# A hybrid encoder layer on one core: the last product of the MLP adds onto accumulator rows placed in PSUM, and the closing norm is reordered

## The chip, the core and the metric

The kernel runs on one core of a Trainium2 chip. The core has five engines that run side by side, each with an instruction queue of its own: TensorE (PE) for matrix products, VectorE (DVE), ScalarE (ACT), GpSimd (POOL) and SyncE (SP), which here only starts transfers. Matrix products write to PSUM, which has eight banks of 128 partitions by 512 fp32; everything else lives in SBUF, and a store to DRAM starts from SBUF. The metric is the device time of one execution in microseconds (us). Before the change it is 755.47 us, the median of three runs (755.42 to 755.72).

## What is computed

One layer over 512 frames of width 1024, in fp32: a gated input projection, forgetting attention and a gated recurrence, an output projection, cross attention to 256 memory tokens, a squared-ReLU MLP with hidden width 4096, and a final RMS norm. Only the end matters here:

```python
u = rmsnorm(h, norm_ff_g[l]) @ w1[l]
h = h + jnp.square(jax.nn.relu(u)) @ w2[l]
return rmsnorm(h, final_norm_g)      # h * rsqrt(mean(h*h) + eps) * g, row by row
```

The output is 512 rows of 1024 numbers, 2 MB.

## The kernel before

Each fp32 operand of a product is split in a high and a low part, and a product is three matmuls (high by high, high by low, low by high). The hidden width is cut into eight groups of 512, numbered g. The MLP's products of group 1 and later use seven products of half-size blocks in place of eight, named "1" to "7" and done in the order 1, 5, 6, 2, 7, 3, 4 (`PRODUCTS`). The weights of each product come as a unit that ACT copies to its high part (line 181, tile `whd`) and DVE subtracts to its low part (line 185, tile `wld`).

The second MLP product is `mlp_down` (line 1528). The last call takes groups 6 and 7 together. A product adds into a pair of PSUM banks, one for each half `t` of 128 rows: `U` for products 1, 6, 7 and 4, `Y` for 5 and 3, `V` for 2. `PLAN` (line 1518) names, for each product, the bank and the quarters of the result that it is added to when it is done. The result is in four tiles `acc[0]` to `acc[3]` of 128 rows by 1024 columns in SBUF; `rows` 0 means tiles 0 and 1, `rows` 1 means tiles 2 and 3, and `half` is the left or right 512 columns. `add_to` (line 1511) is DVE's addition of a bank onto such a quarter. After product 7 the left halves of tiles 2 and 3 lack only what bank `U` holds plus product 4. After product 3 tiles 0 and 1 are complete.

`finish` (line 1635) runs for the products that complete a half of a tile in the last call. The first time for a tile it takes the sum of squares of that half on ACT (line 1641), adds a term for eps on POOL (line 1642) and multiplies the half by the norm's gain `gfin` on POOL (line 1644, tile `fa`). The second time, after product 3, for tiles 0 and 1, it adds the squares of the other half on DVE (`squares`, line 1605) and takes the power -1/2 on POOL (`row_scale`, line 1610, tile `fr`). Tile 0 is scaled and stored at once: `scale_a` on ACT scales the half that was multiplied by the gain already, `dma_a` stores it from ACT's queue, `scale_b` on DVE multiplies the other half by the row factor and the gain and stores it from SP's queue. Tile 1 is put into `deferred`.

`last_product` (line 1566) is product 4. Inside it the order of ACT's and DVE's instructions is the order of the program text; PE's is so everywhere. Elsewhere a scheduler orders ACT, DVE, POOL and the transfers by when it reckons that they can start and by their place in the text. The block does:

- `add_to` of bank `U` for tile 3, then twelve matmuls of 512 columns for tile 2 onto bank `U` (`product`), and `add_to` of that bank onto tile 2;
- scaling and stores of tile 1, and ACT's squares of tile 2 (line 1589);
- for each 256 columns of tile 3: twelve matmuls into a fresh bank `Z`, DVE's addition onto tile 3 (line 1598) and DVE's squares (line 1599);
- `scale_a`, `dma_a`, `scale_b` for tile 2 and then tile 3, with the gain read from a copy in PSUM (`gfin_ps`, lines 1717 and 1718).

The outputs leave in eight transfers of 256 KB, two for each tile, four from ACT's queue and four from SP's. The program's end (line 1744) waits on SP for every transfer and then joins the engines.

Of the kernel before, what the change touches and what calls it, by code (L numbers as in the profile page):

```python
# [46 lines left out]
def emit(  # L47
# [21 lines left out]
    nc = tc.nc  # L69
    te, ve, ac, gp = nc.tensor, nc.vector, nc.scalar, nc.gpsimd  # L70
# [3 lines left out]
    out = out[0]  # L74
# [22 lines left out]
    def s4(shape, name, dt=F32):  # L97
        return s4p.tile([P] + shape, dt, tag="s4", name=name)
# [556 lines left out]
    for hp in range(2):  # L655
        wt = next_panel()
        for j in range(2):
            h = 2 * hp + j
            ps = mm(f"gq{h}")
# [63 lines left out]
    for hp in range(2):  # L723
        Ac.append(t2(f"Ac{hp}", F32, (8, 64)))
        dgs = []
        for h in (2 * hp, 2 * hp + 1):
            dgs.append(sc(f"dg{h}", (4, 64)))
            for c in range(NT):
                for o in (0, 64):
                    cs = slice(c * P + o, c * P + o + 64)  # L730
# [53 lines left out]
    for li, m in enumerate(mlev):  # L784
# [8 lines left out]
        for hp in range(2):  # L793
# [3 lines left out]
            ps = sc(f"lv{hp}{m}", (NT, 2, w))  # L797
# [5 lines left out]
        for hp, ps in enumerate(lvs):  # L803
# [18 lines left out]
            for j in range(2):  # L822
                h = 2 * hp + j
                qv, kv, fv = halves(qt_(h), m), halves(kt_(h), m), halves(F_[:, j, :], m)
# [3 lines left out]
            fv = halves(F_.rearrange("p h t -> p (h t)"), m)  # L828
# [93 lines left out]
    for c in range(NT):  # L922
        cs = slice(c * P, (c + 1) * P)
# [23 lines left out]
        with ahead(P1):  # L947
            hs = sm(4, f"hs{c}")
# [136 lines left out]
    for n in range(len(pairs) + 2):  # L1085
        if n < len(pairs):
            p, tb = pairs[n]
# [165 lines left out]
    acc = []  # L1253
# [53 lines left out]
    HS = S // 2  # L1307
# [196 lines left out]
    def hidden_ahead(key, n, within=None):  # L1504

        used = hb_order.index(key)
        for k in hb_order[used : used + n]:
            if k not in hbs and k[0] in comb and (within is None or k[0] in within):
                hidden_part(*k)

    def add_to(ps, rows, half, t, sign):
        a = acc[2 * rows + t][:, half * S : (half + 1) * S]
        if sign > 0:
            ve.tensor_tensor(a, ps, a, ALU.add)
        else:
            ve.scalar_tensor_tensor(a, ps, -1.0, a, op0=ALU.mult, op1=ALU.add)
# [11 lines left out]
    def mlp_down(gs):  # L1528

        end = gs[-1] == NG - 1  # L1530
        banks = {}
        for n, name in enumerate(PRODUCTS):
            bank, first_, goes = PLAN[name]
            if end and name == PRODUCTS[-1]:
                last_product(gs, banks)
                return
            for g, t in [(g, t) for g in gs for t in range(2)]:
                whi, wlo = unit("d", g, name)
                hidden_ahead((g, name), 1)
                hb = hbs[g, name]  # L1540
                if first_ and g == gs[0]:
                    banks[bank, t] = {"U": sc, "Y": tr}[bank](f"{bank}{g}{t}")
                ps = banks[bank, t]
                ts_ = slice(t * P, (t + 1) * P)
                for k in range(2):
                    hi, lo = hb[:, 0, k, ts_], hb[:, 1, k, ts_]
                    begin = first_ and g == gs[0] and k == 0
                    te.matmul(ps, hi, whi[:, k, :], start=begin, stop=False, skip_group_check=True)  # L1548
                    te.matmul(ps, hi, wlo[:, k, :], start=False, stop=False, skip_group_check=True)  # L1549
                    at = te.matmul(ps, lo, whi[:, k, :], start=False, stop=k == 1, skip_group_check=True)  # L1550
                presum.tick(6 * S / 2400, at)
                if end and (g, t) == (gs[0], 1):
                    hidden_ahead((g, name), HB + 1)
                if g != gs[-1]:
                    continue
                if name == "1":
                    banks["V", t] = mm(f"V{g}{t}")
                    ac.activation(banks["V", t], ps, AF.Copy)
                for rows, half, sign in goes:
                    add_to(ps, rows, half, t, sign)  # L1560
                    if end and (name, rows) in FINAL:
                        finish(2 * rows + t, half)
            hidden_ahead((gs[-1], name), HB, gs)
            yield

    def last_product(gs, banks):

        name = PRODUCTS[-1]

        def steps(g, t, cols):  # L1570
            (whi, wlo), hb = unit("d", g, name), hbs[g, name]
            for k in range(2):
                hi, lo = (hb[:, x, k, t * P : (t + 1) * P] for x in range(2))
                yield from ((hi, whi[:, k, cols]), (hi, wlo[:, k, cols]), (lo, whi[:, k, cols]))

        def product(ps, t, cols, start):
            ops = [op for g in gs for op in steps(g, t, cols)]
            for i, (a, b) in enumerate(ops):
                te.matmul(ps, a, b, start=start and i == 0, stop=i == len(ops) - 1, skip_group_check=True)

        with tc.manual_schedule(engines={mybir.EngineType.Activation, mybir.EngineType.DVE}):
            add_to(banks["U", 1], 1, 0, 1, 1)
            product(banks["U", 0], 0, slice(0, S), False)
            add_to(banks["U", 0], 1, 0, 0, 1)
            o2, o3, v = s4([D], "fo2"), s4([D], "fo3"), fin[3][0]
            _, half1, o1, r1_ = deferred
            scale_a(1, o1, r1_)
            e2 = sm(1, "fv2")
            ac.activation(o2[:, 0:S], acc[2][:, 0:S], AF.Square, scale=1.0 / 32.0, accum_out=e2)
            gp.tensor_tensor(e2, e2, fin[2][0], op=ALU.add)  # L1590
            r2_ = row_scale(e2, "fr2")
            dma_a(1, o1)
            scale_b(1, half1, o1, r1_, gfin[half1])
            for q in range(2):
                qs = slice(q * HS, (q + 1) * HS)
                ps = mm(f"Z{q}")[:, 0:HS]
                product(ps, 1, qs, True)
                ve.tensor_tensor(acc[3][:, qs], ps, acc[3][:, qs], ALU.add)
                v = squares(3, o3, qs, v, f"fv3{q}")
            for tb, o, r in ((2, o2, r2_), (3, o3, row_scale(v, "fr3"))):  # L1600
                scale_a(tb, o, r)
                dma_a(tb, o)
                scale_b(tb, 0, o, r, gfin_ps)

    def squares(tb, o, cs, v0, name):
        a, v = acc[tb][:, cs], sm(1, name)
        ve.tensor_tensor_reduce(out=o[:, cs], in0=a, in1=a, scale=1.0 / D, scalar=v0, op0=ALU.mult, op1=ALU.add, accum_out=v)
        return v

    def row_scale(v, name):  # L1610
        r = sm(1, name)
        gp.tensor_tensor(r, v, mhalf[:, 0:1], op=ALU.pow)
        return r

    def rows_(tb):
        return slice(tb * P, (tb + 1) * P)

    def scale_a(tb, o, r):
        _, cs, ag = fin[tb]
        ac.activation(o[:, cs], ag, AF.Identity, scale=r)  # L1620

    def dma_a(tb, o):
        cs = fin[tb][1]
        ac.dma_start(out[rows_(tb), cs], o[:, cs])

    def scale_b(tb, half, o, r, g):
        cs = slice(half * S, (half + 1) * S)
        ve.scalar_tensor_tensor(o[:, cs], acc[tb][:, cs], r, g, op0=ALU.mult, op1=ALU.mult)
        nc.sync.dma_start(out[rows_(tb), cs], o[:, cs])


    FINAL = (("2", 0), ("7", 1), ("3", 0))
    fin, deferred = {}, []

    def finish(tb, half):

        a = acc[tb]
        cs = slice(half * S, (half + 1) * S)
        if tb not in fin:
            e = sm(1, f"fe{tb}")  # L1640
            ac.activation(t2(f"fj{tb}"), a[:, cs], AF.Square, scale=1.0 / 32.0, accum_out=e)
            gp.tensor_tensor(e, e, eps3[:, tb : tb + 1], op=ALU.add)
            ag = t2(f"fa{tb}")
            gp.tensor_tensor(ag, a[:, cs], gfin[half], op=ALU.mult)
            fin[tb] = (e, cs, ag)
            return
        o = s4([D], f"fo{tb}")
        r = row_scale(squares(tb, o, cs, fin[tb][0], f"fv{tb}"), f"fr{tb}")
        if tb == 1:

            deferred.extend((tb, half, o, r))
            return
        scale_a(tb, o, r)
        dma_a(tb, o)
        scale_b(tb, half, o, r, gfin[half])

    for g in range(1, NG):
        up_units(g)
# [55 lines left out]
                pass  # L1714

    hidden_ahead((NG - 2, PRODUCTS[0]), HB)
    gfin_ps = pvt("gfin_ps")
    ac.activation(gfin_ps, gfin[0], AF.Copy)
    for _ in mlp_down((NG - 2, NG - 1)):
        pass  # L1720

# [27 lines left out]
```

## Time and profile before

| what | value |
|---|---|
| median of three runs | 755.47 us (755.42 to 755.72) |
| the profiled execution's own time | 755.52 us |
| its span, first to last instruction | 753.8 us |
| granted TensorE clock, mean | 0.998 |
| share of PE in the chain that ended last | 95% |

The span is what the profile shows; 1.7 us of the profiled execution's time lie around it. The page of the profile gives busy times of the engines, a picture of the span in 40 slices, and the chain of work that ended last. The trace behind it can be asked for the instructions in order of time (start, duration, engine, line, operation, destination and sources), for the waits, and for each engine's busy time and the transfers' rate in any stretch. An issue is the instruction on an engine's queue that starts a transfer. Times within the span are counted from its start.

### The profile page before, as it was taken

How to read it: one execution, taken by the hardware profiler on the slowest of the kernel's cores; microseconds unless marked ns; L12 is line 12 of the kernel's file. 1: busy time of each engine (PE TensorE's matmuls, PEld its weight loads, DVE VectorE, ACT ScalarE, POOL GpSimd, SP SyncE). 2: the span in 40 equal slices, each digit the busy share in tenths (PEclk: the TensorE clock that was granted, in tenths of full speed). 3: DMA queues.
4: the chain of work that ended last, by engine and by line, in shares of the span. 5: the costliest groups of instructions: out<-in, count | busy, mean ns of one | idle time of the engine just before them, and what ended most of it. 6: DMA issues, size and time to landing. Idle time of an engine off the chain costs nothing.

```text
span 753.8 us, 12203 instructions
## 1 busy us (share of the span) xinstructions
PE 744.8 (99%) x4573; PEld 651.3 (86%) x4573; DVE 539.0 (72%) x849; ACT 434.1 (58%) x721; POOL 202.5 (27%) x278
## 2 busy tenths in 40 slices
PE   9999999999999999999999999999999999999996
PEld 6889788888888988888888889898989899999985
DVE  5647873677878756645546589978788778878797
ACT  5655555655766532334434369757666757574863
POOL 7207531233433237621011211111111111100033
PEclk9999999999999999999999999999999999999999
DMA  8641987567947889985678997998989898968352
GB/s 250 197 117 56 307 264 222 179 227 254 300 175 224 269 219 210 196 164 117 128 174 156 220 209 204 224 230 240 229 205 248 221 241 210 245 194 238 125 113 111
DMA packets 109964, 152.91 MB, mean 203 GB/s; under 512 B 6177, under 2 KB 75850, under 8 KB 109906
## 3 DMA queue, kind: packets, MB, share of 16 engines
q1 hardware_dynamic: 85314, 111.74, 45.9%
q0 software_dynamic: 24000, 39.35, 30.0%
q10 hardware_dynamic: 592, 1.05, 0.4%
q8 instruction: 36, 0.59, 0.3%
q14 instruction: 22, 0.18, 0.1%
HBM read 147.91 MB, written 51.40 MB: 264 GB/s over the span
## 4 chain that ended last, share of the span: by engine, by line
PE 95%; DVE 1%; ACT 1%; POOL 1%; issue 1%; ACTq 0%; POOLq 0%
PE U L1548 4%; PE U L1549 4%; PE U L1550 4%; PE uU L1423 4%; PE uU L1422 4%; PE uU L1421 4%; PE xq L254 2%; PE wo L254 2%; PE xq L255 2%; PE xq L256 2%; PE xw L256 2%; PE xw L255 2%; PE xw L254 2%; PE wo L256 2%; PE wo L255 2%; PE Y L1548 2%
## 5 line engine op out<-in xcount | busy, mean ns | idle before, releaser
L185 DVE TENSOR_TENSOR wld<-wrd,whd 128x1024 fp32r<-128x1024 f32 x56 | 68.3, 1222 | 15.2 <-ACT whd L181 15.1
L185 DVE TENSOR_TENSOR wlu<-wru,whu 128x1024 fp32r<-128x1024 f32 x49 | 59.0, 1218 | 26.6 <-ACT whu L181 26.6
L181 ACT ACTIVATE whu<-wru 128x1024 fp32r<-128x1024 f32 x49 | 51.7, 1060 | 44.6 <-PE U L1550 16.8
L181 ACT ACTIVATE whd<-wrd 128x1024 fp32r<-128x1024 f32 x56 | 58.9, 1052 | 10.9 <-PE uU L1422 4.8
L1548 PE MATMUL U<-whd,hb 128*128 128x512 f32 x120 | 46.8, 390 | 0.0
L1549 PE MATMUL U<-wld,hb 128*128 128x512 f32 x120 | 46.8, 390 | 0.0
L1550 PE MATMUL U<-whd,hb 128*128 128x512 f32 x120 | 46.7, 389 | 0.0
L445 POOL DMA_DIRECT2D wsd<-in_w_dram x16 | 17.4, 1085 | 79.4 <-PE U L1550 15.3
L1015 POOL TENSOR_SCALAR bi<-nF,Ft 128x128 f32<-128x128 f32 (+3 forms) x32 | 21.2, 670 | 59.8 <-PE pt L1047 33.8
L445 POOL DMA_DIRECT2D wsu<-in_w_dram x14 | 17.1, 1218 | 54.6 <-PE xw L256 15.5
L1423 PE MATMUL uU<-x_hi,wlu 128*128 128x256 f32 x112 | 31.7, 283 | 0.0
L1421 PE MATMUL uY<-xs_hi,whu 128*128 128x256 f32 x112 | 31.7, 283 | 0.0
L1422 PE MATMUL uY<-xs_lo,whu 128*128 128x256 f32 x112 | 31.7, 283 | 0.0
L1423 PE MATMUL uY<-xs_hi,wlu 128*128 128x256 f32 x112 | 31.7, 283 | 0.0
L1421 PE MATMUL uU<-xs_hi,whu 128*128 128x256 f32 x112 | 31.7, 283 | 0.0
L1422 PE MATMUL uU<-xs_lo,whu 128*128 128x256 f32 x112 | 31.7, 283 | 0.0
L1423 PE MATMUL uU<-xs_hi,wlu 128*128 128x256 f32 x112 | 31.7, 283 | 0.0
L1422 PE MATMUL uU<-x_lo,whu 128*128 128x256 f32 x112 | 31.7, 283 | 0.0
L1421 PE MATMUL uU<-x_hi,whu 128*128 128x256 f32 x112 | 31.7, 283 | 0.0
L1360 POOL DMA_DIRECT2D wrd<-in_w_dram x8 | 9.7, 1218 | 78.2 <-DVE wld L185 51.1
L1360 POOL DMA_DIRECT2D wru<-in_w_dram x7 | 9.3, 1329 | 68.2 <-DVE wlu L185 68.2
L1158 ACT ACTIVATE x_hi<-hT,gv 128x512 fp32r<-128x512 f32 x16 | 11.4, 715 | 27.5 <-DVE hT L1157 27.5
(965 smaller groups left out, 2659.8 us busy)
## 6 DMA issues: line engine op xcount, KB each, us to landing
wsd<-in_w_dram SPq DMA_DIRECT2D x24, 512.0 KB, 7.5
wrd<-in_w_dram SPq DMA_DIRECT2D x24, 512.0 KB, 5.5
wrd<-wsd SPq DMA_DIRECT2D x24, 512.0 KB, 4.3
wsu<-in_w_dram SPq DMA_DIRECT2D x21, 512.0 KB, 6.1
wru<-in_w_dram SPq DMA_DIRECT2D x21, 512.0 KB, 6.2
wru<-wsu SPq DMA_DIRECT2D x21, 512.0 KB, 5.2
wsd<-in_w_dram POOLq DMA_DIRECT2D x16, 512.0 KB, 7.7
wsu<-in_w_dram POOLq DMA_DIRECT2D x14, 512.0 KB, 7.4
```

What stands on the lines that cost most here:

```text
L181: at = ac.activation(hi, raw, AF.Copy)
L185: ve.tensor_tensor(lo, raw, f(hi), ALU.subtract)
L254: te.matmul(ps, wh, hi, start=n_ == 0 and not begun, stop=False)
L255: te.matmul(ps, wh, lo, start=False, stop=False)
L256: at = te.matmul(ps, wl, hi, start=False, stop=k == order[-1])
L445: yield gp.dma_start(wsum[kind, g, name], src, accum_op=ALU.add, **more)
L1421: te.matmul(ps[:, i, :], whi[:, k, ws], xh[:, k, :], start=begin, stop=False, skip_group_check=True)
L1422: te.matmul(ps[:, i, :], whi[:, k, ws], xl[:, k, :], start=False, stop=False, skip_group_check=True)
L1423: at = te.matmul(ps[:, i, :], wlo[:, k, ws], xh[:, k, :], start=False, stop=k == UK - 1, skip_group_check=True)
L1548: te.matmul(ps, hi, whi[:, k, :], start=begin, stop=False, skip_group_check=True)
L1549: te.matmul(ps, hi, wlo[:, k, :], start=False, stop=False, skip_group_check=True)
L1550: at = te.matmul(ps, lo, whi[:, k, :], start=False, stop=k == 1, skip_group_check=True)
```

## The change

After product 7 of the last call a new function `onto_rows` runs on DVE. It adds the left half of tile 2 onto its bank `U`, in place. It writes the sum of tile 3's bank and the right 256 columns of tile 3's left half to a PSUM bank of its own, and adds the left 256 columns of tile 3's bank onto tile 3 in SBUF. So product 4 of tile 2 ends with the finished rows in its bank, and so does product 4 of the last 256 columns of tile 3; only the first 256 columns of tile 3 are still added by DVE. Squares and scaling read these banks directly.

For tile 0 the squares go from DVE to ACT, and its `scale_b` goes into the block of `last_product`, as all of tile 1's closing does. In the block the order is by hand: product 4 of tile 2; DVE's squares of tile 1; `scale_b` of tile 0; ACT's squares of tile 2's bank; `scale_a`, store and `scale_b` of tile 1; `scale_a` of tile 2, stored from SP's queue; the first 256 columns of tile 3; `scale_b` of tile 2; the last 256 columns with ACT's squares, one DVE addition of the two sums of squares, the power, and the scaling of tile 3. The gain's copy in PSUM is gone.

The stores: `scale_b` of tiles 0 and 1 leaves in three transfers (32, 32 and 64 rows), of tile 2 in two (64 rows each), and of tile 3 in two of 256 columns each. With the four of `scale_a` there are 14 in place of 8; 11 are issued from SP's queue and 3 from ACT's.

```diff
             if end and name == "7":
+                onto_rows(banks)
...
+    def onto_rows(banks):
+        u0, u1, a = banks["U", 0], banks["U", 1], acc[3]
+        ve.tensor_tensor(u0, u0, acc[2][:, 0:S], ALU.add)
+        onto.append(mm("Z1")[:, 0:HS])
+        ve.tensor_tensor(onto[0], u1[:, HS:S], a[:, HS:S], ALU.add)
+        ve.tensor_tensor(a[:, 0:HS], u1[:, 0:HS], a[:, 0:HS], ALU.add)
...
-            add_to(banks["U", 1], 1, 0, 1, 1)
-            product(banks["U", 0], 0, slice(0, S), False)
-            add_to(banks["U", 0], 1, 0, 0, 1)
...
+            u0 = banks["U", 0]
+            product(u0, 0, slice(0, S), False)
+            o2, o3 = s4([D], "fo2"), s4([D], "fo3")
+            (half, o0, r0_), (_, o1, r1_) = deferred
+            hs = slice(half * S, (half + 1) * S)
+            row_scale(r1_, squares(acc[1][:, hs], o1[:, hs], fin[1][0], "fv1"))
+            e2, e3, r2_, r3_ = sm(1, "fv2"), sm(1, "fv3"), sm(1, "fr2"), sm(1, "fr3")
+            scale_b(0, half, o0, r0_)
+            ac.activation(o2[:, 0:S], u0, AF.Square, scale=1.0 / 32.0, accum_out=e2)
+            gp.tensor_tensor(e2, e2, fin[2][0], op=ALU.add)
+            row_scale(r2_, e2)
             scale_a(1, o1, r1_)
...
+            dma_a(ac, 1, o1)
+            scale_b(1, half, o1, r1_)
+            scale_a(2, o2, r2_)
+            dma_a(nc.sync, 2, o2)
+            h0, h1 = slice(0, HS), slice(HS, S)
+            z0, z1 = mm("Z0")[:, 0:HS], onto[0]
+            product(z0, 1, h0, True)
+            ve.tensor_tensor(acc[3][:, h0], z0, acc[3][:, h0], ALU.add)
+            v3 = squares(acc[3][:, h0], o3[:, h0], fin[3][0], "fv30")
+            scale_b(2, 0, o2, r2_, u0)
+            product(z1, 1, h1, False)
+            ac.activation(o3[:, h1], z1, AF.Square, scale=1.0 / 32.0, accum_out=e3)
+            ve.tensor_tensor(e3, e3, v3, ALU.add)
+            row_scale(r3_, e3)
+            scale_a(3, o3, r3_)
+            dma_a(ac, 3, o3)
+            for cs, src in ((h0, acc[3][:, h0]), (h1, z1)):
+                ve.scalar_tensor_tensor(o3[:, cs], src, r3_, gfin[0][:, cs], op0=ALU.mult, op1=ALU.mult)
+                nc.sync.dma_start(out[rows_(3), cs], o3[:, cs])
...
+    def scale_b(tb, half, o, r, src=None):
+        cs = slice(half * S, (half + 1) * S)
+        src = acc[tb][:, cs] if src is None else src
+        ve.scalar_tensor_tensor(o[:, cs], src, r, gfin[half], op0=ALU.mult, op1=ALU.mult)
+        n = P // 4
+        for lo, hi in ((0, n), (n, 2 * n), (2 * n, P)) if tb < 2 else ((0, 2 * n), (2 * n, P)):
+            nc.sync.dma_start(out[tb * P + lo : tb * P + hi, cs], o[lo:hi, cs])
...
+        o, r = s4([D], f"fo{tb}"), sm(1, f"fr{tb}")
+        if tb == 0:
+            v = sm(1, "fv0")
+            ac.activation(o[:, cs], a[:, cs], AF.Square, scale=1.0 / 32.0, accum_out=v)
+            gp.tensor_tensor(v, v, fin[0][0], op=ALU.add)
+            row_scale(r, v)
+            scale_a(0, o, r)
+            dma_a(ac, 0, o)
+        deferred.append((half, o, r))
...
-    gfin_ps = pvt("gfin_ps")
-    ac.activation(gfin_ps, gfin[0], AF.Copy)
```

More of the change, by code (lines that the diff above doesn't have):

```diff
@@ L1562, in mlp_down @@
                         finish(2 * rows + t, half)
+            if end and name == "7":
+                onto_rows(banks)
             hidden_ahead((gs[-1], name), HB, gs)
             yield
+    onto = []
+    def onto_rows(banks):
[4 more added lines that the diff above has]
+        ve.tensor_tensor(a[:, 0:HS], u1[:, 0:HS], a[:, 0:HS], ALU.add)
     def last_product(gs, banks):
@@ L1581, in last_product @@
         with tc.manual_schedule(engines={mybir.EngineType.Activation, mybir.EngineType.DVE}):
-            add_to(banks["U", 1], 1, 0, 1, 1)
-            product(banks["U", 0], 0, slice(0, S), False)
-            add_to(banks["U", 0], 1, 0, 0, 1)
-            o2, o3, v = s4([D], "fo2"), s4([D], "fo3"), fin[3][0]
-            _, half1, o1, r1_ = deferred
-            scale_a(1, o1, r1_)
-            e2 = sm(1, "fv2")
-            ac.activation(o2[:, 0:S], acc[2][:, 0:S], AF.Square, scale=1.0 / 32.0, accum_out=e2)
@@ L1590, in last_product @@
[L1590 to L1603, printed above, removed]
@@ L1605, in squares @@
-    def squares(tb, o, cs, v0, name):
-        a, v = acc[tb][:, cs], sm(1, name)
-        ve.tensor_tensor_reduce(out=o[:, cs], in0=a, in1=a, scale=1.0 / D, scalar=v0, op0=ALU.mult, op1=ALU.add, accum_out=v)
-        return v
-    def row_scale(v, name):
-        r = sm(1, name)
+            u0 = banks["U", 0]
[3 more added lines that the diff above has]
+            hs = slice(half * S, (half + 1) * S)
@@ new lines, in last_product, with squares @@
+            row_scale(r3_, e3)
[4 more added lines that the diff above has]
+                nc.sync.dma_start(out[rows_(3), cs], o3[:, cs])
+    def squares(a, o, v0, name):
+        v = sm(1, name)
+        ve.tensor_tensor_reduce(out=o, in0=a, in1=a, scale=1.0 / D, scalar=v0, op0=ALU.mult, op1=ALU.add, accum_out=v)
+        return v
@@ L1612, in row_scale @@
+    def row_scale(r, v):
         gp.tensor_tensor(r, v, mhalf[:, 0:1], op=ALU.pow)
@@ L1620, in scale_a, with dma_a @@
         ac.activation(o[:, cs], ag, AF.Identity, scale=r)
-    def dma_a(tb, o):
+    def dma_a(queue, tb, o):
         cs = fin[tb][1]
-        ac.dma_start(out[rows_(tb), cs], o[:, cs])
-    def scale_b(tb, half, o, r, g):
+        queue.dma_start(out[rows_(tb), cs], o[:, cs])
+    def scale_b(tb, half, o, r, src=None):
         cs = slice(half * S, (half + 1) * S)
-        ve.scalar_tensor_tensor(o[:, cs], acc[tb][:, cs], r, g, op0=ALU.mult, op1=ALU.mult)
-        nc.sync.dma_start(out[rows_(tb), cs], o[:, cs])
+        src = acc[tb][:, cs] if src is None else src
[3 more added lines that the diff above has]
+            nc.sync.dma_start(out[tb * P + lo : tb * P + hi, cs], o[lo:hi, cs])
     FINAL = (("2", 0), ("7", 1), ("3", 0))
@@ L1646, in finish @@
             return
[L1647 to L1655, printed above, removed]
+        o, r = s4([D], f"fo{tb}"), sm(1, f"fr{tb}")
[7 more added lines that the diff above has]
+        deferred.append((half, o, r))
     for g in range(1, NG):
```

## The prediction

> **What bounds the kernel now.** I read the page first (span, engines, chain), then the chain and the timeline of the last 18 us, then the waits of SP and the rate of the transfers in the tail.
>
> ```profile
> span 753.8 us, 12203 instructions
> PE 744.8 (99%) x4573; PEld 651.3 (86%) x4573; DVE 539.0 (72%) x849; ACT 434.1 (58%) x721; POOL 202.5 (27%) x278
> PE 95%; DVE 1%; ACT 1%; POOL 1%; issue 1%; ACTq 0%; POOLq 0%
> ```
>
> PE is busy for 99% of the span and makes 95% of the chain. The change keeps all its matmuls, so only two things can move: whether PE stays without a gap, and what comes after its last matmul. The chain and the timeline show that end:
>
> ```profile
> 741.32 2.72 PE U L1579 x12
> 744.04 2.88 PE Z L1579 x24
> ...
> 746.95 0.42 DVE L1598 TENSOR_TENSOR acc<-Z,acc 128x256 f32<-128x256 f32 x1 [0.48 <-PE Z L1579]
> 747.16 0.72 ACT L1620 ACTIVATE fo<-fa,fr 128x512 f32<-128x512 f32 x1 [1.01 <-POOL fr L1612]
> 747.40 0.48 DVE L1607 CUSTOM_DVE_ANT_0 fo<-acc,fv 128x256 f32<-128x256 f32 x1
> 747.82 0.08 DVE L1607 DVE_READ_ACCUMULATOR2_ANT fv<- 128x1 f32 x1
> 747.91 0.34 ACTq L1624 DMA_DIRECT2D out_dram<-fo  x1
> 747.98 0.55 POOL L1612 TENSOR_TENSOR fr<-fv,mhalf 128x1 f32<-128x1 f32 x1 [0.85 <-DVE fv L1607]
> ...
> 748.56 0.72 ACT L1620 ACTIVATE fo<-fa,fr 128x512 f32<-128x512 f32 x1 [0.68 <-POOL fr L1612]
> 748.56 0.75 DVE L1628 SCALAR_TENSOR_TENSOR fo<-acc,fr,gfin_ps 128x512 f32<-128x512 f32 x1
> 749.31 0.37 ACTq L1624 DMA_DIRECT2D out_dram<-fo  x1
> 749.33 0.33 SPq L1629 DMA_DIRECT2D out_dram<-fo  x1
> ```
>
> PE's last matmul ends at 746.92 (744.04 + 2.88). Then one thing follows another: addition, squares, reading the sum, power (row factor at 748.53), scaling to 749.31, two issues. The span ends at 753.8, 4.5 us after those issues begin. The rate of the transfers and SP's waits say what these are:
>
> ```profile
> 744.25:744.50 0.25, 0.25 (x5) 0.25 (x4) 0.25 (x1) 0.00 (x0) 0.25 (x1) 1.00 0.53 205
> 748.75:751.50 2.75, 0.00 (x0) 0.00 (x0) 0.55 (x1) 0.53 (x1) 0.00 (x0) 0.85 1.00 374
> 751.50:752.00 0.50, 0.00 (x0) 0.00 (x0) 0.00 (x0) 0.00 (x0) 0.00 (x0) 0.50 0.12 41
> SPq L1744 <- DMA out_dram<-fo: 2.3, 1, 2.3
> L1744 SPq EVENT_SEMAPHORE  x8: 27/28/28, 752.1 to 752.5; - x8
> ```
>
> The last two columns of the first three rows are the share of the 16 transfer engines in use and GB/s. From 748.75 to 751.50 they are full at 374 GB/s: the 1 MB of tiles 2 and 3 goes out without a break and ends at about 751.56 (12% of the next 0.5 us). SP waits 2.3 us for the last transfer to be reported, then goes through eight checks from 752.1 to 752.5, one for each outstanding transfer; the joining of the engines takes the rest, 753.8 - 752.5 = 1.3 us.
>
> **The change, part by part.** Two durations serve several parts. The first pair of stores was issued at 743.47 and 743.50:
>
> ```profile
> 743.47 0.39 ACTq L1624 DMA_DIRECT2D out_dram<-fo  x1
> 743.50 6.17 SPq L1629 DMA_DIRECT2D out_dram<-fo  x4
> ```
>
> The slice from 744.25 is 53% full, so bytes begin at about 744.25 + 0.25 x 0.47 = 744.37, 0.87 after the issue. And 512 KB at 374 GB/s take 1.40 us.
>
> *Seeding the banks.* DVE has three additions more (one of 512 columns, two of 256) and loses the one for tile 3's bank and, later, the one for tile 2's. Its queue around that time:
>
> ```profile
> 737.11 1.27 DVE L1516 SCALAR_TENSOR_TENSOR acc<-U,acc 128x512 f32<-128x512 f32 x2
> 738.31 0.67 DVE L1514 TENSOR_TENSOR acc<-U,acc 128x512 f32<-128x512 f32 x1
> 738.91 1.34 DVE L185 TENSOR_TENSOR wld<-wrd,whd 128x1024 fp32r<-128x1024 f32 x1
> 740.18 0.68 DVE L1516 SCALAR_TENSOR_TENSOR acc<-Y,acc 128x512 f32<-128x512 f32 x1
> 741.88 0.68 DVE L1516 SCALAR_TENSOR_TENSOR acc<-Y,acc 128x512 f32<-128x512 f32 x1
> 742.75 0.39 PE L1579 MATMUL U<-wld,hb 128*128 128x512 f32 x1
> ```
>
> The seeds can start when both product-7 additions are done, at 738.38, which is where the addition for tile 3 stood (738.31). They take 0.67 + 2 x 0.42 = 1.51 us in place of 0.67, so what is behind them on DVE comes 0.84 us later. PE needs bank U at 741.32 in the chain; the first seed is done by 739.0, 2.3 us before. The next in DVE's queue is the low part of the last weight unit (738.91), late by 0.84: done at 741.1. Product 4 reads group 6's weights in its first six matmuls and group 7's low part in its eighth, at 742.75: 1.6 us to spare. Then come the two Y additions, which PE does not wait for. So the seeds cost nothing; PE's six matmuls of product 4 on group 6 and the second half of product 3 cover them. Without that cover each microsecond that the seed is late is a microsecond of PE. Bounds: 0 to +1.4 (the first rival below).
>
> *The closing before PE's end.* The Y additions end at about 741.8 and 742.4. Tile 0's squares move to ACT, then a small addition and the power on POOL:
>
> ```profile
> 745.44 0.61 ACT L1589 ACTIVATE fo<-acc 128x512 f32<-128x512 f32 x1
> 745.96 0.19 ACT L1589 ACTIVATION_READ_ACCUMULATOR fo<-acc 128x1 f32 x1
> 746.29 0.22 POOL L1590 TENSOR_TENSOR fv<-fv,fe 128x1 f32<-128x1 f32 x1 [1.51 <-ACT fo L1589]
> ```
>
> Squares with their read take 0.71 (745.44 to 746.15), the hop 0.14, then 0.22 and 0.55 plus hops: tile 0's factor is there at about 743.5 in place of 742.68, tile 1's at 744.0 in place of 744.78 (744.23 + 0.55 in its own row). On ACT, in the order by hand: scaling tile 0 743.5 to 744.2, its issue to 744.6, squares of tile 2's bank to 745.3, scaling tile 1 to 746.0, its issue (0.35) to 746.4, scaling tile 2 to 747.1. That last one ends 0.2 after PE does, so ACT, which now carries the squares on the chain, may be late by up to 0.2. Tile 2's factor is ready at 745.3 + 0.14 + 0.22 + 0.55 and hops = 746.3, its `scale_b` on DVE done by 747.25, and SP issues its three stores between 747.1 and 748.2 (0.34 each) where before they went at 747.91 and 748.57. All stores ahead of tile 3's are 2 MB x 3/4 at 374 GB/s = 4.2 us of transfer between 744.9 and 749.7; they fit if they run at that rate.
>
> *After PE's end.* Out go the addition (0.42) and DVE's squares with their read (747.40 to 747.90). In come ACT's squares of 256 columns from PSUM with a read, and one DVE addition on a single column. Nearest rows:
>
> ```profile
> L1051 ACT ACTIVATE pts<-pt 128x512 f32<-128x512 f32 x4 | 2.4, 594 | 2.4 <-PE pt L1047 2.4
> L1051 ACT ACTIVATE pts<-pt 128x256 f32<-128x256 f32 x4 | 1.5, 380 | 1.6 <-PE pt L1047 1.6
> L386 DVE TENSOR_TENSOR m0m<-m0m 128x1 f32<-128x1 f32 x1 | 0.2, 160 | 3.5 <-ACT m0j L385 3.5
> L1628 DVE SCALAR_TENSOR_TENSOR fo<-acc,fr,gfin 128x512 f32<-128x512 f32 x2 | 1.5, 752 | 0.2 <-POOL fr L1612 0.2
> ```
>
> From PSUM 256 columns cost 0.21 less than 512, so squares with read take 0.71 - 0.21 = 0.50. From 746.95 that is 747.45, hop 0.05 to 0.14, addition 0.16, hop 0.08, power 0.55: the factor is ready between 748.29 and 748.38 if ACT is free, 0.15 to 0.2 later if it is not. I take 748.43, 0.1 before the 748.53 of today, with bounds 748.3 and 748.6.
>
> *Tile 3's stores.* The multiplication of 256 columns costs 0.75 less the 0.27 by which DVE's 256-column addition is shorter than its 512-column one (0.42 against 0.69, a step that I carry over), 0.48. So the first piece is done at 748.46 + 0.48 = 748.94 and issued at once; ACT's half is issued at 749.2, the second piece at 749.45. Bytes flow from 748.97 + 0.87 = 749.84, and since the others arrive before the first piece's 0.35 us are over and ACT's half lasts 0.70, the 512 KB go out unbroken to 751.24, against 751.56: a gain of 0.32. Bounds: 0.7 (factor at 748.3, no gap behind the first piece and nothing in front) and 0 (the pieces come after older bytes, as today).
>
> *The end.* Eight checks follow the report of the last transfer today, 0.06 us apart. 14 stores share the same waiting list, and where the last one stands in it the trace does not show: between none and all of the 0.5 us is saved. I take the middle, 0.25. The 14 issues against 8 cost SP 3 more before tile 2's, at 0.34 each; DVE and ACT cover them, as SP is idle from 746.4 until tile 2's store in the estimate above. If it were not, tile 3's first piece would come 0.34 later for each issue still in front of it.
>
> *The gain's copy* in PSUM leaves ACT 46 us before the end, off the chain: nothing. Multiplying by the gain from SBUF takes 0.752 where from PSUM it took 0.744: nothing.
>
> *Sum*, against the profiled execution's 755.52: -0.32 for the earlier bytes, -0.25 for the checks, 754.95. That execution is 0.05 above the median, so 754.9.
>
> The rows give 374 GB/s for stores of 128 rows. [...]
>
> **The rivals.** *First, PE waits for its seed: slower.* DVE's queue is in order, and outside the block a scheduler orders it. If the seed of tile 2 goes behind the second Y addition, which cannot start before PE's product 3 ends at 741.32, it is done at 741.32 + 2 x 0.68 = 742.7 and PE stands still for 1.4 us; with tile 1's squares (0.8) ahead of it too, 2.2. Less the 0.6 of the sum, that is 756.3 to 757.1. It decides as soon as DVE starts the seed after 740.6. For it: the seed is new work on a queue that is full from 737.11. Against it: the addition of the same readiness stood at 738.31 today, ahead of the weight split and both Y additions.
>
> *Second, the pieces run at half rate: slower.* If stores of 32 and 64 rows move at 187 GB/s and hold the engines while they do, a tile costs 0.70 + 1.40 = 2.1 us, tiles 0 to 2 end at 744.9 + 6.3 = 751.2 and tile 3 at 752.6 in place of 751.56: +1.0 - 0.25, 756.2. It decides once the first three tiles end after 749.84, that is above 1.65 us for a tile. Against it: pieces of different rows and ACT's halves are under way together.
>
> *Third, no gain.* ACT arrives late at the last squares, or tile 3's first piece waits on SP for an earlier store, and the checks save nothing: 755.3 to 755.6.
>
> *Fourth, twice the gain.* Factor at 748.3, bytes ending 0.7 earlier, all of the checks saved: 754.3.
>
> **How the numbers follow.** Forecast 0.58, first rival 0.08, second 0.08, third 0.16, fourth 0.10. The likeliest time is 754.9, its own range 754.5 to 755.2. For 8 in 10 I reach down to 753.9, a little past the fourth, and up to 756.1, short of the first and about half of the second. 0.2% is 1.51 us, about what a measurement of this kernel can tell from no change: 753.96 and 756.98. Faster than that would need more than the fourth rival's 1.2 us, 0.08; slower needs the upper end of the first, 0.07; within, 0.85.
>
> **What would show it.** Bank U seeded by 739 and no gap in PE at 741; the last low weight part done near 741.1; ACT's last squares starting within 0.2 us of 746.95; tile 3's factor near 748.4; stores issued there from about 749.0 and full transfer engines until about 751.2; fewer than eight checks after the last report. I am wrong if PE has a gap before product 4, if the stores of tiles 0 to 2 are still moving at 749.8, or if the time moves by more than 1.5 us, for which nothing here has a price.

## The result, and the profile after

The changed kernel takes 757.39 us, the median of nine runs (757.05 to 757.78), against 755.31 for the kernel before (754.87 to 755.72): a ratio of 1.0028, 95% interval 1.0018 to 1.0038. It is slower by 2.1 us, where 754.9 was forecast and 753.9 to 756.1 was the range.

The page of the changed kernel, then its chain of waits near the end (start, duration, what):

```profile
span 756.1 us, 12215 instructions
PE 745.0 (99%) x4573; PEld 651.4 (86%) x4573; DVE 537.5 (71%) x847; ACT 434.9 (58%) x724; POOL 202.6 (27%) x279
PE 92%; DVE 3%; ACT 2%; issue 1%; POOL 1%; POOLq 0%; ACTq 0%; DVEq 0%
...
738.61 0.60 DVE U L1573
739.21 0.33 DVE Z L1575
739.54 0.32 DVE acc L1576
739.87 1.85 DVE wld L185
741.71 0.61 DVE acc L1516
...
742.35 0.73 ACT fo L1673 x2
...
743.22 0.65 POOL fv L1674
...
743.94 0.59 POOL fr L1632
...
744.55 0.73 ACT fo L1640
```

PE's busy time is the same to 0.2 us. What changed is who stands in the chain: before, PE led it to its last matmul. Now it runs through the three seeds on DVE, the weight split, tile 0's squares on ACT, POOL's addition and power, and tile 0's scaling. By this chain the end hangs on tile 0's closing, which had been work beside PE. The chain ends on DVE at 750.3 and does not follow the stores, which go on for some four microseconds more. So I read each run by its tail, from the end of PE's last matmul to the end of the span. The last matmuls of before and after are these:

```profile
746.63 0.28 PE L1579 MATMUL Z<-whd,hb 128*128 128x256 f32 x1
```

```profile
746.84 0.28 PE L1591 MATMUL Z<-whd,hb 128*128 128x256 f32 x1
```

They end at 746.91 and 747.12, and the other runs have PE's end between 746.2 and 747.3, so the 0.2 is scatter. The tail was 753.8 - 746.9 = 6.9 us and is now 756.1 - 747.1 = 9.0. The timeline of that tail in the changed kernel:

```profile
745.33 3.28 SPq L1652 DMA_DIRECT2D out_dram<-fo  x6
747.52 0.72 ACT L1640 ACTIVATE fo<-fa,fr 128x512 f32<-128x512 f32 x1 [0.47 <-POOL fr L1632]
748.15 0.36 ACT L1617 ACTIVATE fo<-Z 128x256 f32<-128x256 f32 x1
748.71 0.53 SPq L1644 DMA_DIRECT2D out_dram<-fo  x1
748.88 0.54 POOL L1632 TENSOR_TENSOR fr<-fv,mhalf 128x1 f32<-128x1 f32 x1 [1.39 <-DVE fv L1618]
749.34 1.25 SPq L1652 DMA_DIRECT2D out_dram<-fo  x2
749.45 0.48 DVE L1623 SCALAR_TENSOR_TENSOR fo<-acc,fr,gfin 128x256 f32<-128x256 f32 x1 [0.66 <-POOL fr L1632]
750.20 0.34 ACTq L1644 DMA_DIRECT2D out_dram<-fo  x1
750.69 1.55 SPq L1624 DMA_DIRECT2D out_dram<-fo  x2
```

Two things are late. ACT takes the last squares at 748.15, 1.0 us after PE is done, because it scales tile 2 first, from 747.52; tile 3's row factor is ready at 749.42. And SP issues stores without a break from 745.33 to 752.24: tile 3's first piece is multiplied by 749.93 and issued at 750.69, its second by 750.34 and issued after 751.2. How long an issue takes, and how fast the bytes move, stands in the stores' own row and in the table by stretch (share of the transfer engines and GB/s last):

```profile
L1652 SPq DMA_DIRECT2D out_dram<-fo x8: 357/504/732, 745.3 to 749.9; - x8
DMA to landing us min/median/max: 3.3/3.5/3.7
746.50:747.00 0.50, 0.50 (x6) 0.42 (x4) 0.33 (x2) 0.50 (x1) 0.40 (x2) 1.00 0.93 217
746.25:753.75 7.50, 0.87 (x8) 0.67 (x6) 2.33 (x7) 2.61 (x7) 1.43 (x3) 0.83 0.88 271
```

An issue of a row piece takes 0.50 us in the median and up to 0.73, against 0.34 before; a store is reported 3.5 us after it, against 2.2. In the first full half microsecond the transfer engines are 93% busy and yet move 217 GB/s. In every half microsecond from 746.50 to 753.50 they are 78 to 100% busy and move 217 to 324 GB/s, pieces and whole stores together; before, full engines moved 374.

### The profile page after: what moved, and what is told of

Read it like the earlier page. It is cut to its first block, busy times and chain, and to the rows that moved or that the text cites. A ratio compares the mean times of both kernels' runs of the same rounds, so it can differ in the third digit from the quotient of the medians.

```text
span 756.1 us, 12215 instructions
## 1 busy us (share of the span) xinstructions
PE 745.0 (99%) x4573; PEld 651.4 (86%) x4573; DVE 537.5 (71%) x847; ACT 434.9 (58%) x724; POOL 202.6 (27%) x279
## 4 chain that ended last, share of the span: by engine, by line
PE 92%; DVE 3%; ACT 2%; issue 1%; POOL 1%; POOLq 0%; ACTq 0%; DVEq 0%
PE uU L1423 4%; PE uU L1422 4%; PE uU L1421 4%; PE U L1548 3%; PE U L1549 3%; PE U L1550 3%; PE xq L254 2%; PE wo L254 2%; PE xq L255 2%; PE xq L256 2%; PE xw L256 2%; PE xw L255 2%; PE xw L254 2%; PE wo L255 2%; PE wo L256 2%; PE uY L1423 2%
```

## The experiments

Ten runs, in three groups. The time of before is that of its runs on the same chip in the same group. The tail is worked out as above from each profiled execution, which is not always the median one: that of e2 is the fastest of its ten, that of e3 the slowest.

| kernel | time, us | before, us | difference | tail, us |
|---|---|---|---|---|
| before | 755.31 | | | 6.9 |
| after | 757.39 | 755.31 | +2.08 | 9.0 |
| e1_rows_whole | 755.72 | 755.35 | +0.37 | 7.3 |
| e2_split_in_before | 756.01 | 755.35 | +0.66 | 7.5 |
| e3_rows_interleaved | 756.15 | 755.35 | +0.80 | 7.8 |
| e4_squares_first | 756.98 | 755.35 | +1.63 | 8.6 |
| e5_whole_squares_first | 755.40 | 755.34 | +0.06 | 7.0 |
| e6_tile0_on_dve | 755.82 | 755.34 | +0.48 | 7.0 |
| e7_seeds_in_before | 756.26 | 755.34 | +0.92 | 7.8 |
| e8_no_pool_product | 756.25 | 755.34 | +0.91 | 8.1 |
| e9_tile3_from_act | 756.98 | 755.47 | +1.51 | 8.8 |
| e10_late_seeds | 754.69 | 755.47 | -0.78 | 6.3 |

The tails follow the times to 0.4 us, so the larger differences lie behind PE's last matmul. For e1, e5 and e6, whose differences are of that size or below, the tails do not show where they lie.

### Whole stores in the changed kernel (e1)

```diff
-        n = P // 4
-        for lo, hi in ((0, n), (n, 2 * n), (2 * n, P)) if tb < 2 else ((0, 2 * n), (2 * n, P)):
-            nc.sync.dma_start(out[tb * P + lo : tb * P + hi, cs], o[lo:hi, cs])
+        nc.sync.dma_start(out[rows_(tb), cs], o[:, cs])
```

> The changed kernel, with scale_b of tiles 0, 1 and 2 stored whole (256 KB each, 9 stores in all); seeds, order and tile 3's two column pieces stay. Theory S (the stores by row ranges fill SP's queue and slow the transfers): SP has four issues fewer, each near 0.35 us, the first piece of tile 3 is issued when its data is ready (about 749.95 in the span), bytes end near 752.2, time about 755.9. Theory C (ACT reaches the last squares late, and that alone sets the end): the row factor of tile 3 stays at 749.4 and the time at 757.4.

755.72, ratio to before 1.0006 (0.9997 to 1.0016): 1.7 us of the 2.1 are gone with five row pieces fewer (three stores in place of eight; the expectation's "four issues fewer" was a miscount). Stores of 128 rows move at the old rate and are issued at about the old pace:

```profile
746.00:748.50 2.50, 0.77 (x7) 0.57 (x5) 1.40 (x4) 1.77 (x5) 0.91 (x2) 1.00 1.02 383
L1650 SPq DMA_DIRECT2D out_dram<-fo x3: 356/357/504, 745.0 to 748.4; - x3
749.62 0.81 SPq L1624 DMA_DIRECT2D out_dram<-fo  x2
```

383 GB/s, 0.36 us for an issue in the median (one of the three took 0.50), and tile 3's first piece goes at 749.62 as soon as it is multiplied. The row factor is as late as in the changed kernel (2.3 us after PE's end in both), and yet only 0.37 is left of the 2.08.

### The split alone, in the kernel before (e2)

```diff
+        if tb == 3:
+            for q in range(2):
+                qs = slice(q * HS, (q + 1) * HS)
+                nc.sync.dma_start(out[rows_(tb), qs], o[:, qs])
+            return
-        nc.sync.dma_start(out[rows_(tb), cs], o[:, cs])
+        n = P // 4
+        for lo, hi in ((0, n), (n, 2 * n), (2 * n, P)) if tb < 2 else ((0, 2 * n), (2 * n, P)):
+            nc.sync.dma_start(out[tb * P + lo : tb * P + hi, cs], o[lo:hi, cs])
```

> The kernel before, with only its stores split as in the change (scale_b of tiles 0 and 1 in 32, 32 and 64 rows, of tile 2 in 64 and 64, of tile 3 in two column halves). Theory S: issues on SP grow to 0.5 us and more, the transfers are slower than 374 GB/s, and it is slower than before by 0.5 to 1.5 us: 755.8 to 756.8. Theory C: the order of before keeps its row factor at 748.5, so the time stays at 755.3.

756.01, ratio 1.0009 (1.0000 to 1.0019): the split costs 0.66, at the edge of what the runs can tell, in the order of before, where the first store is issued 3.4 us ahead of PE's end and not 1.8. An early half microsecond shows the same sign, busy engines and few bytes:

```profile
744.00:744.50 0.50, 0.50 (x6) 0.50 (x5) 0.46 (x2) 0.37 (x1) 0.10 (x1) 1.00 0.94 217
```

### As many pieces, of interleaved rows (e3)

```diff
-        n = P // 4
-        for lo, hi in ((0, n), (n, 2 * n), (2 * n, P)) if tb < 2 else ((0, 2 * n), (2 * n, P)):
-            nc.sync.dma_start(out[tb * P + lo : tb * P + hi, cs], o[lo:hi, cs])
+        for lo, step in ((0, 4), (2, 4), (1, 2)) if tb < 2 else ((0, 2), (1, 2)):
+            nc.sync.dma_start(out[tb * P + lo : (tb + 1) * P : step, cs], o[lo:P:step, cs])
```

> The changed kernel with as many stores of the same sizes, but each takes every fourth or every second row (32, 32 and 64 rows; 64 and 64) in place of a range of rows. [...] If the number of stores on one queue is what costs, it stays at 757.4, with issues on SP of 0.5 us and more.

756.15, ratio 1.0011 (1.0001 to 1.0020): 1.24 less than the changed kernel (its slowest run, 756.84, is below the changed kernel's fastest, 757.05), with the same number of stores, the same sizes and the same order. Only which rows go together differs:

```profile
746.50:747.00 0.50, 0.50 (x6) 0.50 (x6) 0.47 (x3) 0.50 (x3) 0.29 (x1) 1.00 1.03 393
747.50:748.00 0.50, 0.00 (x0) 0.00 (x0) 0.27 (x1) 0.27 (x1) 0.20 (x1) 1.00 0.17 57
749.50:750.00 0.50, 0.00 (x0) 0.00 (x0) 0.33 (x1) 0.34 (x1) 0.13 (x1) 1.00 0.13 45
L1651 SPq DMA_DIRECT2D out_dram<-fo x8: 478/590/601, 745.5 to 750.6; - x8
DMA to landing us min/median/max: 2.3/2.3/2.3
```

In the half microsecond in which the changed kernel moved 217 GB/s this one moves 393, and a store is reported after 2.3 us. So it is the range of rows that lowers the rate, not the size or the number. But the second and third rows have the engines nearly idle: SP needs 0.59 us for an issue, while a piece of 64 or 128 KB moves in 0.17 or 0.33 us at that rate, so SP does not feed them. The expectation came true in part: the issues on SP stay long, but the time did not stay at 757.4. The rate is that of whole stores, and what the pieces cost by their number is 756.15 - 755.72 = 0.43, with overlapping intervals. Why a range of rows moves more slowly, no run shows.

### The last squares ahead of tile 2's scaling (e4)

```diff
-            scale_a(2, o2, r2_)
-            dma_a(nc.sync, 2, o2)
...
             ac.activation(o3[:, h1], z1, AF.Square, scale=1.0 / 32.0, accum_out=e3)
+            scale_a(2, o2, r2_)
+            dma_a(nc.sync, 2, o2)
```

> The changed kernel with ACT's squares of the last 256 columns put ahead of the scaling of tile 2. Theory C: the squares start at 747.5 in place of 748.15, tile 3's row factor comes 0.65 us earlier, and so does the end: 756.7. Theory S: SP's queue holds older stores until 750.6 anyway, so tile 3's pieces are issued no earlier and the time stays within 0.2 of 757.4.

756.98: 0.41 less than the changed kernel, with overlapping intervals, and between the two theories (0.65 and 0.2). The trace shows why it is neither:

```profile
747.20 0.38 ACT L1615 ACTIVATE fo<-Z 128x256 f32<-128x256 f32 x1 [0.42 <-PE Z L1591]
750.41 1.51 SPq L1624 DMA_DIRECT2D out_dram<-fo  x2
```

PE ends at 746.84 here. The squares start 0.36 us later, behind ACT's issue of tile 1's store (746.81 to 747.15), and tile 3's factor comes 0.46 earlier against PE's end, not 0.65. Tile 3's pieces leave SP no earlier than in the changed kernel, 3.57 us after PE's end in both, as theory S had it. Only ACT's half of tile 3 is issued earlier against PE's end, by 0.45.

### Whole stores and squares first (e5)

The two diffs of e1 and e4 together.

> The changed kernel with both edits at once: scale_b of tiles 0 to 2 stored whole, and ACT's squares of the last 256 columns ahead of the scaling of tile 2. With whole stores alone it took 755.72, and there tile 3's row factor set the issue of its first piece. If the late squares are what is left (theory C for the rest), the factor comes 0.65 us earlier and so does the end: 755.1, a little under before's 755.35. If the transfers bound it even with whole stores, it stays at 755.7.

755.40, ratio 1.0003 (0.9994 to 1.0011), 0.06 above before. The factor came 0.52 earlier (the power ends 748.55 in place of 749.07 in e1), and the median fell by 0.32, half of what was expected; the intervals of the two runs overlap. These two edits bring the changed kernel back to before, and not under it.

### Tile 0's squares back on DVE (e6)

```diff
-            v = sm(1, "fv0")
-            ac.activation(o[:, cs], a[:, cs], AF.Square, scale=1.0 / 32.0, accum_out=v)
-            gp.tensor_tensor(v, v, fin[0][0], op=ALU.add)
-            row_scale(r, v)
+            row_scale(r, squares(a[:, cs], o[:, cs], fin[0][0], "fv0"))
```

> The version with whole stores and squares first, and tile 0's squares back on DVE (as before the change). If moving them to ACT and POOL is what makes tile 0's factor 1.0 us late, the factor comes near 743.5 in place of 744.5 and tile 0's and 1's stores start earlier; ACT is then free at PE's end, but since the squares of the last columns already wait for PE in the version before it, the time changes by less than 0.3: 754.8 to 755.1.

755.82 against 755.40: no gain, and rather a loss, though the intervals overlap. Tile 0's factor came 0.65 us earlier against PE's end, so moving the squares was part of why it was late. But DVE did the squares before the second Y addition, and what follows on DVE came later: tile 1's squares end at 744.71 in place of 743.41 in e5. The tail is 7.0 us in both, so the earlier factor of tile 0 bought nothing at the end.

### The seeds alone, in the order of before (e7)

The kernel before with `onto_rows` after product 7, product 4 onto the seeded banks, tile 2's squares and scaling from its bank, the last squares on ACT, and eight whole stores:

```diff
-            add_to(banks["U", 1], 1, 0, 1, 1)
-            product(banks["U", 0], 0, slice(0, S), False)
-            add_to(banks["U", 0], 1, 0, 0, 1)
+            u0 = banks["U", 0]
+            product(u0, 0, slice(0, S), False)
...
+            ac.activation(o2[:, 0:S], u0, AF.Square, scale=1.0 / 32.0, accum_out=e2)
...
+            scale_a(2, o2, r2_)
+            dma_a(2, o2)
...
+            product(z1, 1, h1, False)
+            ac.activation(o3[:, h1], z1, AF.Square, scale=1.0 / 32.0, accum_out=e3)
```

> The kernel before with the seeded banks alone: tile 0 closed at once with DVE's squares, eight whole stores, tile 2's squares taken from its bank. If the idea of the change is sound and only its stores and its order cost, tile 3's row factor is ready 0.2 us earlier against PE's end than before, tile 2's stores leave earlier, and it takes 754.8 to 755.2 against 755.35. If the three seeds on DVE delay the closing by themselves, it is at 755.4 or above.

756.26, ratio 1.0013 (1.0004 to 1.0022): slower by 0.9 without one store more. So the stores are not all of it. But this run does not show that the seeds cost by themselves, for ACT's order differs too: ACT scales tile 2 and issues its store ahead of the last squares.

```profile
748.27 0.38 ACT L1615 ACTIVATE fo<-Z 128x256 f32<-128x256 f32 x1 [0.47 <-ACT fo L1639]
```

PE ends at 747.01. The squares start 1.26 us later, and tile 3's factor is ready 2.55 us after PE's end, where before the change it took 1.62. These 0.93 us match the loss of 0.92. e5, with the same three seeds and the squares first, is level with before. What the seeds do shows in tile 0's factor, 3.2 us ahead of PE's end in place of 4.2; some of ACT's lateness may come from there. The next run asks why it is late, and e10 what that is worth.

### No product on POOL beside the split (e8)

```diff
-            ag = t2(f"fa{tb}")
-            gp.tensor_tensor(ag, a[:, cs], gfin[half], op=ALU.mult)
-            fin[tb] = (e, cs, ag)
+            ag = t2(f"fa{tb}") if tb < 2 else None
+            if tb < 2:
+                gp.tensor_tensor(ag, a[:, cs], gfin[half], op=ALU.mult)
+            fin[tb] = (e, cs, ag if tb < 2 else a[:, cs])
```

> The changed kernel without POOL's product of the right halves of tiles 2 and 3 with the gain, so their outputs lack that factor. In the changed kernel the last weight split on DVE took 1.93 us and POOL's first small addition 0.64, where before they took 1.34 and 0.22. If DVE's split is long because POOL works on SBUF beside it, it takes 1.25 or less here and tile 0's factor comes at least 0.6 us earlier. If it is long for a reason of DVE's own (the seeds before it), it stays near 1.9. The time moves little, since the stores stay as they are: 756.8 to 757.4.

First the changed kernel, then this one, at the last weight split:

```profile
738.09 2.55 POOL L1667 TENSOR_TENSOR fa<-acc,gfin 128x512 f32<-128x512 f32 x2 [2.37 <-DVE acc L1516]
739.79 1.93 DVE L185 TENSOR_TENSOR wld<-wrd,whd 128x1024 fp32r<-128x1024 f32 x1
743.22 0.64 POOL L1674 TENSOR_TENSOR fv<-fv,fe 128x1 f32<-128x1 f32 x1 [1.31 <-ACT fo L1673]
```

```profile
739.34 1.21 DVE L185 TENSOR_TENSOR wld<-wrd,whd 128x1024 fp32r<-128x1024 f32 x1
742.05 0.71 POOL L1675 TENSOR_TENSOR fv<-fv,fe 128x1 f32<-128x1 f32 x1 [2.85 <-ACT fo L1674]
742.84 1.11 POOL L1632 TENSOR_TENSOR fr<-fv,mhalf 128x1 f32<-128x1 f32 x2
```

Without POOL's product the split takes 1.21, as did the split ahead of it in the changed kernel (736.20). With it beside, 1.93. But POOL's products lay over the split before the change as well, from end to end, and there it took 1.34 (738.91 to 740.25):

```profile
737.87 3.53 POOL L1644 TENSOR_TENSOR fa<-acc,gfin 128x512 f32<-128x512 f32 x2 [2.37 <-DVE acc L1516]
```

So the difference is not how much of POOL lies beside it, but where the split starts. Before, it starts 0.26 us ahead of the end of POOL's first product (737.87 to 739.17). The split takes 1.34, and the second product, which starts under it, takes 2.27 where the first took 1.30. In the changed kernel the seeds push the split to 739.79, 0.84 us ahead of the end of the second product (740.63), and it is the split that takes long, while both products take 1.30. In both it ends 1.08 or 1.09 us after the product that was under way when it started. That fits a split that waits for that product; the rows show no wait as such.

POOL's addition for tile 0 stays long (0.71): it starts while DVE takes tile 1's squares and ends just after them (742.05 to 742.76, the squares with their read 741.96 to 742.71), so the product was not its cause. The time fell to 756.25, by 1.1 us, more than the 0.6 expected at the most: SP's run of issues starts with tile 0's factor, here 0.65 us earlier against PE's end, and it ends 0.60 earlier. The rest of the 1.1 is not explained.

### Tile 3's pieces from ACT's queue (e9)

```diff
-                nc.sync.dma_start(out[rows_(3), cs], o3[:, cs])
+                ac.dma_start(out[rows_(3), cs], o3[:, cs])
```

> The changed kernel with tile 3's two column pieces issued from ACT's queue, behind ACT's own store of tile 3; all other stores and sizes as in the change. In the changed kernel SP issues its eleven stores back to back from 745.3 to 752.2, and these two are the last. If that queue's pace sets the end, they are issued by 751.3 in place of 752.2 and the time falls by about 0.9, to 756.5. If the slow moving of the row ranges sets it, the bytes still wait and the time stays within 0.3 of 757.4.

756.98, 0.41 less than the changed kernel; taken against before in each group, 0.57 less; the intervals overlap. That is between the two answers. The first piece left 3.54 us after PE's end in place of 3.57 and the last issue ended 4.93 after it in place of 5.12, so the other queue gained little and the run does not settle which of the two it is.

```profile
L1624 ACTq DMA_DIRECT2D out_dram<-fo x2: 411/647/883, 749.9 to 750.4; - x2
```

ACT's issues of these pieces take 0.41 and 0.88, where its whole stores take 0.34 to 0.41. Long issues are therefore not a property of SP's queue; what makes them long was not found.

### Only one seed ahead of the split (e10)

```diff
     def onto_rows(banks):
-        u0, u1, a = banks["U", 0], banks["U", 1], acc[3]
+        u0 = banks["U", 0]
         ve.tensor_tensor(u0, u0, acc[2][:, 0:S], ALU.add)
-        onto.append(mm("Z1")[:, 0:HS])
-        ve.tensor_tensor(onto[0], u1[:, HS:S], a[:, HS:S], ALU.add)
-        ve.tensor_tensor(a[:, 0:HS], u1[:, 0:HS], a[:, 0:HS], ALU.add)
...
             row_scale(r1_, squares(acc[1][:, hs], o1[:, hs], fin[1][0], "fv1"))
+            onto.append(mm("Z1")[:, 0:HS])
+            ve.tensor_tensor(onto[0], banks["U", 1][:, HS:S], acc[3][:, HS:S], ALU.add)
+            ve.tensor_tensor(acc[3][:, 0:HS], banks["U", 1][:, 0:HS], acc[3][:, 0:HS], ALU.add)
```

with whole stores and squares first as in e5.

> The version with whole stores and squares first, with only the seed of tile 2's bank ahead of the last weight split; the two for tile 3 come behind DVE's squares of tile 1. If the seeds push the split into POOL's work on SBUF, the split takes 1.3 or less here, tile 0's factor comes 1.0 us earlier against PE's end, and tiles 0 to 2 are stored sooner; tile 3's factor stays 1.5 us after PE's end, so at most 0.3 is gained at the end: 755.0 to 755.4. If tile 0's factor is late for another reason, it is as the version before it, 755.4.

754.69 against 755.47: ratio 0.9990 (0.9981 to 0.9999), faster than both kernels, and 0.3 below the 755.0 that was expected at the best. Its timeline:

```profile
737.61 3.54 POOL L1665 TENSOR_TENSOR fa<-acc,gfin 128x512 f32<-128x512 f32 x2 [2.37 <-DVE acc L1516]
738.05 0.68 DVE L1573 TENSOR_TENSOR U<-U,acc 128x512 f32<-128x512 f32 x1
738.65 1.34 DVE L185 TENSOR_TENSOR wld<-wrd,whd 128x1024 fp32r<-128x1024 f32 x1
741.50 0.19 POOL L1672 TENSOR_TENSOR fv<-fv,fe 128x1 f32<-128x1 f32 x1
741.76 0.58 POOL L1632 TENSOR_TENSOR fr<-fv,mhalf 128x1 f32<-128x1 f32 x1
746.68 0.38 ACT L1615 ACTIVATE fo<-Z 128x256 f32<-128x256 f32 x1 [1.57 <-PE Z L1588]
747.43 0.54 POOL L1632 TENSOR_TENSOR fr<-fv,mhalf 128x1 f32<-128x1 f32 x1 [2.04 <-DVE fv L1618]
```

The split is back at 1.34. It was not moved out of POOL's work, as its expectation had it: it lies under POOL's products from end to end, but again starts 0.26 us ahead of the end of the first one (738.91), and it is the second that takes long. POOL's addition is back at 0.19, since it now falls before DVE's squares (they start at 741.93) and not under them. Tile 0's factor is ready at 742.34, 4.3 us before PE's end (746.65); in the changed kernel it was 2.6 before. ACT waits 1.57 us for PE's last matmul, and tile 3's factor is ready at 747.97, 1.3 us after PE's end, where before the change it took 1.6 and in e5 1.8. In e5 ACT was still issuing tile 1's store when PE ended, and DVE had tile 2's scaling ahead of the addition of the two sums; here both are done in time. The idea of the change, rows placed in the banks, is worth 0.3 us of factor; it came out only with two of its seeds behind the split, whole stores and the last squares first. How much of the 0.78 is the factor and how much the earlier stores of tiles 0 to 2, no run separates.

## Why the prediction was wrong, step by step

*What bounds the kernel.* The reading held for the kernel before and PE stayed without a gap. That the end would go on hanging on PE's end was taken for granted, and it fell: the chain of the changed kernel leaves PE and goes through tile 0's closing, and the transfer engines are 88% busy from 746.25 to 753.75.

*Seeding the banks.* "The seeds cost nothing" held for PE, and the first rival did not come. The term that failed is what comes behind them: "late by 0.84: done at 741.1". The 0.84 was a little too much: the split began 0.67 later (739.79 less 738.91, less 0.21 by which PE's work itself lies later). The miss is its duration: it took 1.93 and ended at 741.72. The 1.34 was carried over as if it were the split's own. e8, e10 and the rows of before show that it depends on where the split starts within POOL's products. That the work after the seeds is "which PE does not wait for" was the wrong question: SP's stores wait for it.

*The closing before PE's end.* Tile 0's factor was put at 743.5 and came at 744.52: 0.6 from the split, 0.4 from POOL's addition (0.64, not 0.22), which fell under DVE's squares (743.06 to 743.81 with their read). ACT's lateness of "up to 0.2" became 1.0, since each of ACT's steps in the order by hand follows the one before. The mechanism was seen, its size was not. Putting the last squares first gained 0.41 in the changed kernel (e4) and 0.32 with whole stores (e5), both with overlapping intervals.

*The stores.* This is the step that failed most: the sum of the prediction has no term for the pieces. Two sentences carry that. "They fit if they run at that rate": with row ranges among the stores the tail moves 271 GB/s, not 374. And "at 0.34 each ... as SP is idle from 746.4": an issue took 0.50 in the median, so SP had no idle time until 752.24. This is the largest part: 1.24 us for the ranges (changed kernel less e3) and 0.43, less certain, for the number of pieces (e3 less e1). The second rival had the rate, with 0.08 of the chances; its condition, the first three tiles still moving at 749.84, came true. Its own sum moves 2 MB in 6.3 + 1.4 us, 272 GB/s, and the tail has 271. No run shows its 187 GB/s for the pieces alone, half of 374: in the changed kernel pieces and whole stores together moved 217 GB/s in the first full half microsecond and 271 over the tail. What its 756.2 lacked is the start: the first stores are issued at 745.30 and 745.33, so bytes flow from about 746.2 in place of 744.9. I let one sentence against it (pieces of different rows are under way together) stand in for a row. The trace had none for it, so both bounds of the rate belonged in the term. With the rival's rate and tile 0's factor 1.0 later the sum would have been 757.2.

*The end.* The checks: 0.25 was taken for them. In the changed kernel the last store that is reported is the last in the list:

```profile
L1765 SPq EVENT_SEMAPHORE  x9: 27/28/28, 752.3 to 754.8; - x9
```

The checks are strung out while stores come in, and the last one, at 754.8, has only the joining behind it, 1.3 us. From the report of the last store to the end it is 1.3 us in place of 1.7 (753.8 - 752.1), so 0.4 was saved, on a tail that was longer by 2.1.

*Tile 3's stores* were issued at 750.69 and 751.32 in place of 748.94 and 749.45. *The gain's copy*: nothing showed.

## What to carry to other kernels

When a bound is nearly all one engine, the work beside its last microseconds is covered only until it ends: before lengthening it, follow it to the stores and see what is left between its end and theirs. If a store has to be split, take interleaved rows and not ranges of neighbouring partitions (756.15 us against 757.39 here), and only where the queue has time for the issues; here no split by rows gained anything. A duration from the trace holds for the neighbours it had there and for its place among them, above all for DVE beside POOL: the same weight split took 1.21, 1.34 or 1.93 us here.

## What the runs showed of the hardware

With stores of ranges of 32 and 64 partitions under way the transfer engines were 93% busy at 217 GB/s in the first full half microsecond and 88% busy at 271 over the tail; with rows 2 or 4 apart they moved 393 in that half microsecond. Issues took 0.34 us before the change, and 0.36 to 0.93 in the changed kernel's pieces; why stays open, as e3 has long ones at full rate too. DVE's split of 128 by 1024 took 1.21 us without POOL's product, and beside POOL's products 1.34 or 1.93 by where it started.
